# Storing a 16 KB result in two halves of 64 partitions, from SyncE and from ScalarE, in place of one store from SyncE

## The chip, the cores and the metric

One core of a Trainium2 chip. The metric is the device time of one execution in microseconds; a time quoted for a kernel is the median of several executions. Each experiment ran beside executions of the kernel before on the same chip. "Tail" means throughout: the time from the end of VectorE's last instruction to the end of the span, read from the trace of one profiled execution. It is the only stretch that the change touches, and in a trace it can be read to a few hundredths of a microsecond, while the whole time scatters by some tenths. The other terms: an "issue" is the time in which an engine's sequencer works on its store instruction. Beside the 128 rows of the store the trace has 16 closing writes of 4 bytes, and 16 "arrivals" are counted at the semaphore; with the last one the store has landed, and the time from the last row to it is called the confirmation.

## The reference

```python
batch, dim_i, dim_j, dim_k = 32, 256, 256, 128
x, y: (batch, 256) f32;  weight: (dim_k, dim_i, dim_j) f32      # 33.5 MB of weight
return np.einsum('bi,bj,kij->bk', x, y, weight)                 # (32, 128) f32: 16 KB
```

## The kernel before

The weight streams in through GpSimd's DMA queue and is cast to bf16 on the way; TensorE multiplies it with a block form of `x`, VectorE multiplies with `y` and sums. The result collects in `acc`: 128 partitions (a batch row and one of four groups of k on each), 32 numbers of 4 bytes on a partition. Partition p of `acc` is bytes 128p to 128p+127 of the result, so the store moves 128 rows of 128 bytes. The last unit's sum and the store:

```python
acc = sbuf("acc", [P, G], f32)                 # 128 x 32
# ... the last unit of weight rows:
done(v.tensor_tensor_reduce(
    out=prod[:, 0, :], in0=sums[:, 0, :], in1=y4, scale=1.0, scalar=0.0,
    op0=mult, op1=add, accum_out=acc[:, unit[0]:unit[0] + 1],
)._wait_ge(s_pe, n_pe))
# ...
out_v = out.rearrange("b (kk g) -> b kk g", kk=KK)
sp.dma_start(out=out_v, in_=acc)._wait_ge(s_dve, n_dve).then_inc(s_out, 16)
sp.sem_inc(s_fin, 1)
pool.wait_ge(s_fin, 1)
pool.dma_reset(range(nums[0], nums[-1] + 1))
pool.sem_clear(range(nums[0], nums[-1] + 1))
sp.wait_ge(s_out, 16)
sp.sem_clear(s_out)
```

SyncE waits for VectorE's last count, issues the store, tells GpSimd that it may clear the semaphores, then waits for the landing. ScalarE loads `x` and 1 MB of weight at the start, casts 2 MB, and has nothing to do after about 11 us.

Of the kernel before, what the change touches and what calls it, by code (L numbers as in the profile page):

```python
# [36 lines left out]
def kernel(  # L37
# [8 lines left out]
    P = 128  # L46
# [6 lines left out]
    B, I = x.shape  # L53
# [12 lines left out]
    def sbuf(name, shape, dtype):  # L66
        return nc.alloc_sbuf_tensor(name, shape, dtype).ap()

    def rows_of(groups):


        step = G // len(groups)
        assert all(g == groups[0] + n * step for n, g in enumerate(groups))
        v = weight.rearrange("(u s) (ip ic) j -> s ip u (ic j)", s=step, ic=IC)
        return v[groups[0]]

    def w_of(groups):
        at = [place_of[g] for g in groups]
        step = at[1] - at[0] if len(at) > 1 else 1
        assert all(a == at[0] + n * step for n, a in enumerate(at))  # L80
        return w_sb[:, at[0]:at[-1] + 1:step, :]
# [14 lines left out]
    acc = sbuf("acc", [P, G], f32)  # L96
# [6 lines left out]
        for s, (groups, lo, hi) in zip(s_w, LOADS) for g in groups for ic in range(lo, hi)  # L103
# [7 lines left out]
    s_dve = nc.alloc_semaphore("dve")  # L111
    s_fin = nc.alloc_semaphore("fin")
    s_out = nc.alloc_semaphore("out")
# [7 lines left out]
            out=w_of(groups)[:, :, lo * J:hi * J],  # L121
            in_=rows_of(groups)[:, :, lo * J:hi * J],
# [9 lines left out]
    for n, (g, queue) in enumerate(zip(FIRST, (nc.sync, nc.scalar))):  # L132
        hw.append(
            queue.dma_start(
                out=w_f[:, n:n + 1, :], in_=rows_of((g,)),
# [13 lines left out]
    for blk in blocks:  # L149
# [15 lines left out]
    pool, act, v, pe, sp = nc.gpsimd, nc.scalar, nc.vector, nc.tensor, nc.sync  # L165
# [4 lines left out]
        out=ident, in_=ident, compare_op=mybir.AluOpType.not_equal, fill=1.0,  # L170
# [13 lines left out]
    n_dve = 0  # L184

    def done(ins):
# [6 lines left out]
        out=x_rep,  # L193
        in_=x_sb.rearrange("b (ip ic) -> b ic ip", ic=IC).unsqueeze(3)
        .to_broadcast([B, IC, IP, KK]),
    )._wait_ge(s_x, 16))
    for q in range(Q):
        c = v.transpose(  # L198
            out=xt[q * 32:(q + 1) * 32, :, :],
            in_=x_rep[:, :, q * IP // Q:(q + 1) * IP // Q, :],  # L200
# [5 lines left out]
        out=mask, in_=ident.rearrange("p (ip kk) -> p kk ip", kk=KK), axis=AX, op=add,  # L206
    )._wait_ge(s_pool, 2))

    for kk in range(KK):
        c = v.tensor_scalar(  # L210
            out=xblk[:, :, :, kk], in0=xt, scalar1=mask[:, kk:kk + 1],
# [8 lines left out]
        out=yt, in_=y_sb.rearrange("b (jb j) -> b jb j", j=32),  # L220
    )._wait_ge(s_y, 16))
    t = done(v.tensor_copy(  # L222
        out=y_rep, in_=yt.unsqueeze(3).to_broadcast([B, J // 32, B, KK]),
    )._wait_ge(s_dve, t))
    BQ = B // Q
    for q in range(Q):
        c = v.transpose(  # L227
            out=y4[q * 32:(q + 1) * 32, :].rearrange("p (jb j) -> p jb j", j=32),
            in_=y_rep[:, :, q * BQ:(q + 1) * BQ, :],
# [22 lines left out]
    for u, unit in enumerate(UNITS):  # L252
# [40 lines left out]
        if n_g > 1:  # L293
            t = done(v.tensor_tensor(  # L294
                out=prod, in0=sums, in1=y4.unsqueeze(1).to_broadcast([P, n_g, J]), op=mult,
# [3 lines left out]
                out=acc[:, unit[0]:unit[-1] + 1:unit[1] - unit[0]], in_=prod, axis=AX, op=add,  # L299
            )._wait_ge(s_dve, t))  # L300
        else:
            done(v.tensor_tensor_reduce(  # L302
                out=prod[:, 0, :], in0=sums[:, 0, :], in1=y4, scale=1.0, scalar=0.0,
# [4 lines left out]


    out_v = out.rearrange("b (kk g) -> b kk g", kk=KK)  # L310
    sp.dma_start(out=out_v, in_=acc)._wait_ge(s_dve, n_dve).then_inc(s_out, 16)
    sp.sem_inc(s_fin, 1)
    pool.wait_ge(s_fin, 1)
    pool.dma_reset(range(nums[0], nums[-1] + 1))
    pool.sem_clear(range(nums[0], nums[-1] + 1))
    sp.wait_ge(s_out, 16)
    sp.sem_clear(s_out)


# [28 lines left out]
```

## Time and profile before

| | before |
|---|---|
| time, first three runs | 84.69, 84.77, 85.2 us; median 84.77 |
| span of the profiled run | 83.37 us |
| VectorE's last instruction ends | 81.87 us |
| tail | 1.50 us |
| from issue of the store to its landing | 1.4 us |

The first 81.9 us are set by the weight stream and what hangs on its last pieces; the tail is the store. The lines that show this are in the prediction below.

### The profile page before, as it was taken

To read this page: it belongs to the slowest core of one execution; us is meant where nothing else is said; L and a number is where in the kernel's file an instruction comes from. 1 tells how busy PE (TensorE), PEld (TensorE's weight loads), DVE (VectorE), ACT (ScalarE), POOL (GpSimd) and SP (SyncE) were. 2 spreads that over 40 slices of the span, in tenths; PEclk is the share of its full clock that TensorE was granted. 3 is DMA by queue.
4 is the path that set the end of the run, shared out by engine and by line. 5 is a ranking of instruction groups with operands and counts; after the bars stand their busy time and mean duration, and the time that the engine had idled before them with its cause. 6 is when DMAs were issued, how large, how long until landed. Compare 5 with 4: busy or idle time off the path is not lost.

```text
span 83.4 us, 257 instructions
## 1 busy us (share of the span) xinstructions
PE 32.5 (39%) x136; PEld 4.3 (5%) x43; DVE 25.2 (30%) x28; ACT 5.2 (6%) x5; POOL 8.8 (11%) x18
## 2 busy tenths in 40 slices
PE   0000000000000000000099999996029999884780
PEld 0000000000000000000000000000000110112330
DVE  0009450000292000000000000003999800999932
ACT  0019930000000000000000000000000000000000
POOL 5999600000000000000000000000000000000000
PEclk9999999999999999999999999999995799999998
DMA  4999999999999999999999999999999999999980
GB/s 122 393 370 293 214 214 212 216 218 212 218 218 216 212 216 216 212 218 214 212 214 218 210 220 214 214 214 216 212 214 218 212 214 216 212 216 214 197 118 8
DMA packets 4912, 17.91 MB, mean 215 GB/s; under 512 B 384, under 2 KB 800, under 8 KB 4656
## 3 DMA queue, kind: packets, MB, share of 16 engines
q0 software_dynamic: 4432, 15.76, 94.4%
q1 hardware_dynamic: 288, 1.07, 3.5%
q10 hardware_dynamic: 192, 1.08, 3.3%
HBM read 33.62 MB, written 0.02 MB: 403 GB/s over the span
## 4 chain that ended last, share of the span: by engine, by line
DMA 46%; PE 39%; DVE 6%; POOL 3%; another core or an unknown queue 3%; issue 2%; POOLq 0%
DMA w_sb<-in_weight_dram 46%; PE ps L237 39%; DVE tmp L294 5%; POOL w_sb L120 2%; POOL y_sb L127 1%; DVE tmp L302 1%; POOL const-float32-0.0 L332 0%; POOLq L332 0%; POOL const-uint8-127 L332 0%; POOL const-float32-1.0 L332 0%; DVE acc L302 0%
## 5 line engine op out<-in xcount | busy, mean ns | idle before, releaser
L237 PE MATMUL ps<-w_sb,xblk 128*128 128x512 bf16 (+1 forms) x136 | 32.5, 396 | 48.9 <-DMA w_sb<-in_weight_dram 44.2
L294 DVE TENSOR_TENSOR tmp<-ps,y 128x4096 f32<-128x4096 f32 (+3 forms) x4 | 8.6, 2156 | 36.7 <-PE ps L237 36.6
L298 DVE TENSOR_REDUCE acc<-tmp 128x16 f32<-128x4096 f32 (+3 forms) x4 | 8.6, 2154 | 0.1
L237 PEld LDWEIGHTS ps<-w_sb,xblk 128*128 128x128 bf16 x43 | 4.3, 101 | 76.9 <-DMA w_sb<-in_weight_dram 42.7
L120 POOL DMA_DIRECT2D w_sb<-in_weight_dram x11 | 7.6, 707 | 0.6 <-issue 0.6
L178 ACT CAST w_sb<-w_f 128x1024 bf16<-128x1024 f32 x4 | 3.9, 1040 | 0.0
L219 DVE STREAM_TRANSPOSE yt<-y_sb 32x256 f32<-32x256 f32 x1 | 0.4, 433 | 10.9 <-DMA y_sb<-in_y_dram 10.9
L192 DVE COPY x_rep<-x_sb 32x1024 f32<-32x1024 f32 x1 | 0.8, 790 | 6.1 <-PEq L332 6.1
L227 DVE STREAM_TRANSPOSE y<-y_rep 32x256 f32<-32x256 f32 x4 | 1.7, 435 | 0.1
L198 DVE STREAM_TRANSPOSE xt<-x_rep 32x256 f32<-32x256 f32 x4 | 1.7, 435 | 0.1
L178 ACT ACT_TABLE_LOAD x1 | 1.3, 1283 | 6.0 <-PEq L332 6.0
L210 DVE TENSOR_SCALAR xblk<-xt,mask 128x256 bf16<-128x256 f32 x4 | 1.4, 499 | 0.0
L302 DVE CUSTOM_DVE_ANT_0 tmp<-ps,y 128x256 f32<-128x256 f32 x2 | 0.8, 424 | 1.6 <-PE ps L237 1.6
L222 DVE COPY y_rep<-yt 32x1024 f32<-32x1024 f32 x1 | 0.7, 682 | 0.0
L205 DVE TENSOR_REDUCE mask<-ident 128x4 f32<-128x128 f32 x1 | 0.4, 382 | 1.0 <-POOL ident L169 1.0
L127 POOL DMA_DIRECT2D y_sb<-in_y_dram x1 | 0.5, 534 | 0.0
L168 POOL MEMSET ident<- 128x128 f32 x1 | 0.3, 302 | 0.0
L169 POOL TENSOR_SCALAR_AFFINE_SELECT ident<-ident 128x128 f32<-128x128 f32 x1 | 0.3, 287 | 0.1
L302 DVE DVE_READ_ACCUMULATOR2_ANT acc<- 128x1 f32 x2 | 0.2, 84 | 0.0
L332 POOL MEMSET const-float32-0.0<- 128x1 f32 x1 | 0.1, 98 | 0.2 <-issue 0.2
L332 POOL MEMSET const-bfloat16-1.0<- 128x1 bf16 x1 | 0.1, 101 | 0.0
L332 POOL MEMSET const-uint8-127<- 128x1 uint8 x1 | 0.1, 101 | 0.0
(1 smaller groups left out, 0.1 us busy)
## 6 DMA issues: line engine op xcount, KB each, us to landing
w_sb<-in_weight_dram POOLq DMA_DIRECT2D x2, 4096.0 KB, 48.0
w_sb<-in_weight_dram POOLq DMA_DIRECT2D x2, 2048.0 KB, 43.3
w_sb<-in_weight_dram POOLq DMA_DIRECT2D x2, 1024.0 KB, 40.9
w_f<-in_weight_dram SPq DMA_DIRECT2D x1, 1024.0 KB, 4.9
w_f<-in_weight_dram ACTq DMA_DIRECT2D x1, 1024.0 KB, 8.3
w_sb<-in_weight_dram POOLq DMA_DIRECT2D x1, 512.0 KB, 72.1
w_sb<-in_weight_dram POOLq DMA_DIRECT2D x1, 256.0 KB, 72.7
w_sb<-in_weight_dram POOLq DMA_DIRECT2D x1, 128.0 KB, 72.9
```

The source lines that it names most:

```text
L120: nc.gpsimd.dma_start(out=w_of(groups)[:, :, lo * J:hi * J], in_=rows_of(groups)[:, :, lo * J:hi * J],).then_inc(s, 16).ins
L127: sw.insert(2, nc.gpsimd.dma_start(out=y_sb, in_=y).then_inc(s_y, 16).ins)
L178: c = act.copy(out=w_sb[:, place_of[g], lo:hi], in_=w_f[:, n, lo:hi])
L192: t = done(v.tensor_copy(out=x_rep, in_=x_sb.rearrange("b (ip ic) -> b ic ip", ic=IC).unsqueeze(3) .to_broadcast([B, IC, IP, KK]),)._wait_ ...
L198: c = v.transpose(out=xt[q * 32:(q + 1) * 32, :, :], in_=x_rep[:, :, q * IP // Q:(q + 1) * IP // Q, :],)
L210: c = v.tensor_scalar(out=xblk[:, :, :, kk], in0=xt, scalar1=mask[:, kk:kk + 1], scalar2=None, op0=mult,)
L222: t = done(v.tensor_copy(out=y_rep, in_=yt.unsqueeze(3).to_broadcast([B, J // 32, B, KK]),)._wait_ge(s_dve, t))
L227: c = v.transpose(out=y4[q * 32:(q + 1) * 32, :].rearrange("p (jb j) -> p jb j", j=32), in_=y_rep[:, :, q * BQ:(q + 1) * BQ, :],)
L237: return pe.add_instruction(mybir.InstMatmult(name=nc.get_next_instruction_name(), engine=mybir.EngineType.PE, ins=[pe.lower_ap(rhs), pe.l ...
L294: t = done(v.tensor_tensor(out=prod, in0=sums, in1=y4.unsqueeze(1).to_broadcast([P, n_g, J]), op=mult,)._wait_ge(s_pe, n_pe))
L298: done(v.tensor_reduce(out=acc[:, unit[0]:unit[-1] + 1:unit[1] - unit[0]], in_=prod, axis=AX, op=add,)._wait_ge(s_dve, t))
L302: done(v.tensor_tensor_reduce(out=prod[:, 0, :], in0=sums[:, 0, :], in1=y4, scale=1.0, scalar=0.0, op0=mult, op1=add, accum_out=acc[:, uni ...
```

## The change

The intent: two engines issue half a store each at the same moment, so that each half is ready sooner.

```diff
-    sp.dma_start(out=out_v, in_=acc)._wait_ge(s_dve, n_dve).then_inc(s_out, 16)
+    act.dma_start(out=out_v[B // 2:], in_=acc[P // 2:, :])._wait_ge(s_dve, n_dve).then_inc(s_out, 16)
+    act.sem_inc(s_fin, 1)
+    sp.dma_start(out=out_v[:B // 2], in_=acc[:P // 2, :])._wait_ge(s_dve, n_dve).then_inc(s_out, 16)
     sp.sem_inc(s_fin, 1)
-    pool.wait_ge(s_fin, 1)
+    pool.wait_ge(s_fin, 2)
     ...
-    sp.wait_ge(s_out, 16)
+    sp.wait_ge(s_out, 32)
```

## The prediction

> **What bounds the kernel now.** The question put to each view was: how much of the time lies behind the last addition, because only that stretch can change. I read first the page's header and slices, then the chain of waits, then the timeline of the last microseconds, then the waits of SyncE, and last the engine table cut into short windows. First the page.
>
> ```profile
> span 83.4 us, 257 instructions
> PE   0000000000000000000099999996029999884780
> DMA  4999999999999999999999999999999999999980
> GB/s 122 393 370 293 214 214 212 216 218 212 218 218 216 212 216 216 212 218 214 212 214 218 210 220 214 214 214 216 212 214 218 212 214 216 212 216 214 197 118 8
> ```
>
> Look at the DMA row: from the second slice to the 38th the DMA engines are at 90% or more, at some 215 GB/s, and TensorE starts only in the second half. The weight stream sets the pace; each slice is 2.1 us, so the stream's end falls near 81 us. The last slice, with DMA 0 and 8 GB/s, is where the result leaves. The chain of waits shows what stands between the stream and that slice:
>
> ```profile
> 3.18 38.65 DMA w_sb<-in_weight_dram
> 41.87 15.66 PE ps L237 x64
> ...
> 81.12 0.30 PE ps L237
> 81.42 0.02 issue
> 81.44 0.42 DVE tmp L302
> 81.86 0.01 DVE acc L302
> ```
>
> The reader should see that the chain ends at 81.87 us, on VectorE, while the span is 83.4 us (83.37 in the trace). The remaining 1.5 us belong to the store, which the chain does not list because a store is no counted work. The changed lines act on these 1.5 us, 1.8% of the 84.77 us. The timeline and SyncE's own waits fill them:
>
> ```profile
> 81.79 0.08 DVE L302 DVE_READ_ACCUMULATOR2_ANT acc<- 128x1 f32 x1
> 81.90 0.35 SPq L311 DMA_DIRECT2D out_dram<-acc  x1
> SPq L317 <- DMA out_dram<-acc: 1.0, 1, 1.0
> out_dram<-acc SPq DMA_DIRECT2D x1, 16.0 KB, 1.4
> ```
>
> SyncE issues for 0.35 us, then waits 1.0 us for the landing; from issue to landing it is 1.4 us for 16 KB. Cutting that stretch into windows shows when bytes move (columns: window, length, busy times, then granted clock, DMA share, GB/s):
>
> ```profile
> 81.90:82.25 0.35, 0.00 (x0) 0.00 (x0) 0.00 (x0) 0.00 (x0) 0.00 (x0) 1.00 0.00 0
> 82.25:82.72 0.47, 0.00 (x0) 0.00 (x0) 0.00 (x0) 0.00 (x0) 0.00 (x0) 1.00 0.00 0
> 82.72:82.98 0.26, 0.00 (x0) 0.00 (x0) 0.00 (x0) 0.00 (x0) 0.00 (x0) 0.71 0.42 63
> 82.98:83.33 0.35, 0.00 (x0) 0.00 (x0) 0.00 (x0) 0.00 (x0) 0.00 (x0) 0.50 0.00 0
> ```
>
> So: 0.02 us from VectorE's end to the issue, 0.35 us issue, 0.47 us with no byte moving, 0.26 us in which all 128 rows of 128 bytes go, 0.35 us from the last row to the semaphore, 0.04 us until SyncE has cleared it. Sum 1.49 us. Bytes move in only 0.26 of it, and even there the 16 engines are busy 0.42 of the time, 0.11 us each (8 rows of 13 ns in the trace's packet records). Behind the span comes a fixed remainder: the profiled run took 84.67 us for 83.37 us of span, 1.30 us.
>
> **What the Trainium skill says.** Four places bear on it.
> "DMA: Bandwidth & Descriptors", section "Rules for kernel authors", has this very change: two transfers to disjoint partition halves, "Don't bother — they serialize", because both halves spread over all 16 DMA engines. Its section "Issuing engines are not separate DMA queues" allows one saving: issuing from several engines "will only save the time on the sequencer it takes to initiate the DMA". Section "Anatomy of one DMA" puts nearly all of a transfer's fixed cost (about 2 us there, for transfers issued by GpSimd) into waiting for the write to be confirmed, not into moving bytes. The trace agrees in kind: 16 KB take 1.4 us, of which 0.26 move data; but the confirmation, 0.35 us, is the smaller part here, and issue plus the silent gap, 0.82 us, the larger.
> "Perfetto Trace Analysis", section "Per-instruction lifecycle", says that the block which writes the descriptors is shared by the two issuing sequencers and locked for one DMA at a time, and that this lock wait lies inside the reported issue window. Whether two issues lengthen each other here is the open question. At the start of this trace SyncE issues from 0.00 for 0.63 us and ScalarE from 0.12 for 0.42 us; they overlap, and ScalarE ends first. So a long strict exclusion is not what is seen, but 0.42 us for only 32 rows, against 0.35 us for the lone store's 128, would fit some mutual hindrance (or the cold start of both).
>
> **The change part by part.**
> Removed: nothing but the size of SyncE's store, 128 rows to 64. Its issue could get shorter if the 0.35 us grew with rows. The trace speaks against much of that: 32 rows took 0.42 us, 128 rows 0.35, 0.56 and 0.63 us. No order by rows is in these four. I put the saving at 0 to 0.05 us.
> Added: one issue on ScalarE of 64 rows. ScalarE's last counted instruction (a cast) ends at about 11.2 us, so its store instruction stands waiting for VectorE's last count for 70 us, as SyncE's does, and both should be released together at about 81.90 us. It lies beside SyncE's issue, so its cost on the path is 0 unless they hinder each other.
> The silent gap, 0.47 us: paid by both stores at once; no saving, it is latency.
> The data: each engine still gets 8 rows, now 4 from each queue, plus 2 closing semaphore writes in place of 1 (9 ns each in the packet records). 0.26 us stays 0.26, perhaps 0.27 us. At the kernel's start, ScalarE's 1 MB transfer sent its first packet at 4.19 us, just as SyncE's 1 MB was sending its last (4.22 us): two queues ran one after the other, not side by side. For 4 rows an engine that makes no sum smaller.
> The confirmation, 0.35 us: the wait is now for the later of two transfers, so the larger of two such latencies counts. Of one transfer's sixteen arrivals the trace has the first at 83.15 and the last at 83.33 us; a maximum over 32 instead of 16 lands a few hundredths later: plus 0 to 0.05 us.
> Moved: GpSimd now clears semaphores after both issues. In the trace it does so from 82.33 to 82.59 us, with SyncE busy waiting until 83.33; it has 0.7 us to spare, so a slightly later start costs nothing.
> Untouched: all up to 81.87 us, and the 1.30 us behind the span.
> Sum: 0 to -0.05 (issue), 0 (gap), +0.01 (data), 0 to +0.05 (confirmation): about 0.00 us if the two issues run freely side by side.[...]
>
> **The rivals.**
> First: the two issues truly overlap and both issue and gap are shorter for 64 rows. For it: a half has half the descriptors to write, and part of the 0.82 us before the first byte may be that writing. Against it: the issue lengths show no such order. If issue and gap both shrank by a quarter it would be -0.2 us, 84.57 us. I give this, or part of it, 20%.
> Second: the lock makes the later store wait for the earlier one. Then the second issue ends up to one issue later: at worst +0.35 us, 85.12 us, and more likely a part of it, +0.1 to +0.2 us. For it: the skill's shared block, and the 0.42 us for 32 rows. Against it: the overlap at the start. I give 35% to some visible hindrance.
> Third: nothing to see, the change drowns in the scatter between runs (84.69 to 85.2 us, 0.5 us among three runs of one kernel): 45%.
> A fourth, that GpSimd's clearing becomes the end, would need its start delayed by more than its 0.7 us of slack; under 3%.
> What none of these can do is reach 2%, 1.70 us: the whole stretch that is touched is 1.49 us, so even a store costing nothing would not do it, and a doubled store (two in strict sequence, issue to landing 1.4 us twice) would be +1.4 us, still within.
>
> **Range and chances.** Weighted: 0.20 × -0.15 + 0.35 × +0.17 + 0.45 × 0 = +0.03, plus the few hundredths for the later of two landings: +0.05 us, so 84.82 us. The mechanism alone spans about -0.2 to +0.35 us; run scatter of the weight stream's end adds some 0.2 us either way, and a median of few runs keeps part of that. I take 84.50 to 85.20 us for 8 in 10. Faster by over 2% (under 83.07 us): 1%. Slower by over 2% (over 86.47 us): 1%, for a different state of the chip rather than for the change. Within 2%: 98%.
>
> **What would show each step right or wrong.** The page should list two issues with 8 KB each, one of SPq and one of ACTq, starting within 0.05 us of each other at about 0.02 us after VectorE's end. Packets should rise by exactly 16, from 4912 to 4928: the rows are the same 128, and one more set of closing writes is added (queue q1 down by 64 to 224, q10 up by 80 to 272). If both issues last about 0.35 us, hindrance is refuted; if one lasts 0.5 us or more, or starts its bytes only when the other's are done with a gap, the second rival is shown. The data phase should stay within 0.23 to 0.35 us at GB/s like before's 63. SyncE's wait for the landing should be 0.9 to 1.2 us. The tail from VectorE's end to the span's end should be 1.4 to 1.8 us, against 1.49. What would make the prediction wrong: a chain up to VectorE's end that differs by more than 0.3 us from 81.87 (then the stream moved, which the change does not explain), a silent gap that grows well over 0.47 us when two queues start at once, or an issue on ScalarE late by more than 0.2 us because its sequencer is slower to wake after 70 us.

## The result, and the profile after

The changed kernel took 85.39 us (median of 6 runs, 85.29 to 85.49), the kernel before 84.80 us (6 runs, 84.69 to 85.2). The ratio is 1.0062, with a 95% interval from 1.0039 to 1.0084: slower by about 0.5 us, small but clear. All six runs were fast, that is, none was over 1.5% above the fastest.

The timeline's last lines and SyncE's wait, after:

```profile
81.96 0.08 DVE L302 DVE_READ_ACCUMULATOR2_ANT acc<- 128x1 f32 x1
82.07 0.52 SPq L313 DMA_DIRECT2D out_dram<-acc  x1
82.07 0.55 ACTq L311 DMA_DIRECT2D out_dram<-acc  x1
SPq L319 <- DMA out_dram<-acc: 1.4, 1, 1.4
out_dram<-acc SPq DMA_DIRECT2D x1, 8.0 KB, 1.7
out_dram<-acc ACTq DMA_DIRECT2D x1, 8.0 KB, 2.0
```

Both engines start together, 0.03 us after VectorE's end, as they should. But each issue now takes 0.52 or 0.55 us where the whole store's took 0.35, and half the bytes take 1.7 and 2.0 us to land where the whole took 1.4. The windows of the tail (columns as in the prediction):

```profile
82.07:82.62 0.55, 0.00 (x0) 0.00 (x0) 0.00 (x0) 0.00 (x0) 0.00 (x0) 1.00 0.00 0
82.62:83.24 0.62, 0.00 (x0) 0.00 (x0) 0.00 (x0) 0.00 (x0) 0.00 (x0) 1.00 0.00 0
83.24:83.45 0.21, 0.00 (x0) 0.00 (x0) 0.00 (x0) 0.00 (x0) 0.00 (x0) 1.00 0.27 39
83.45:83.51 0.06, 0.00 (x0) 0.00 (x0) 0.00 (x0) 0.00 (x0) 0.00 (x0) 1.00 0.00 0
83.51:83.72 0.21, 0.00 (x0) 0.00 (x0) 0.00 (x0) 0.00 (x0) 0.00 (x0) 1.00 0.28 39
83.72:84.06 0.34, 0.00 (x0) 0.00 (x0) 0.00 (x0) 0.00 (x0) 0.00 (x0) 1.00 0.00 0
```

Rows move twice, in two bursts with a pause of 0.06 us between them. By the packet records the first burst is SyncE's and the second ScalarE's. Counted from VectorE's end:

| | before | after | difference |
|---|---|---|---|
| first row leaves | 0.871 us | 1.203 us | +0.332 |
| first row to end of the last closing write | 0.234 us | 0.477 us | +0.243 |
| last closing write to last arrival at the semaphore | 0.349 us | 0.336 us | -0.013 |
| last arrival to end of span | 0.042 us | 0.046 us | +0.004 |
| tail | 1.496 us | 2.062 us | +0.566 |

The 0.566 us are the whole of the ratio (0.62% of 84.8 us is 0.53 us). VectorE's end also lies 0.17 us later in this trace (82.04 against 81.87), but so does the landing of the last weights (81.24 against 81.07); over the fifteen profiled runs that add nothing to the weight stream VectorE's end falls between 81.74 and 82.22 us, so that is scatter of the stream. GpSimd's clearing ends 0.92 us after VectorE's end, over a microsecond before the span's end.

From here on "last row" includes its closing write, which ends 5 to 6 ns after the rows.

Three questions follow. Why is the first row later? Why do two halves not move side by side? And is either a matter of two engines at all?

### The profile page after: what moved, and what is told of

Read it like the earlier page. It is cut to its first block, busy times and chain, and to the rows that moved or that the text cites. A ratio compares the mean times of both kernels' runs of the same rounds, so it can differ in the third digit from the quotient of the medians.

```text
span 84.1 us, 259 instructions
## 1 busy us (share of the span) xinstructions
PE 33.4 (40%) x136; PEld 4.3 (5%) x43; DVE 25.0 (30%) x28; ACT 5.3 (6%) x5; POOL 8.8 (10%) x18
## 2 busy tenths in 40 slices
DMA packets 4928, 17.91 MB, mean 213 GB/s; under 512 B 400, under 2 KB 816, under 8 KB 4672
## 4 chain that ended last, share of the span: by engine, by line
DMA 46%; PE 40%; DVE 6%; POOL 3%; another core or an unknown queue 2%; issue 1%; POOLq 0%
DMA w_sb<-in_weight_dram 46%; PE ps L237 40%; DVE tmp L294 5%; POOL w_sb L120 2%; POOL y_sb L127 1%; DVE tmp L302 1%; POOL const-float32-0.0 L334 0%; POOLq L334 0%; POOL const-uint8-127 L334 0%; POOL const-float32-1.0 L334 0%; DVE acc L302 0%
## 5 line engine op out<-in xcount | busy, mean ns | idle before, releaser
L237 PE MATMUL ps<-w_sb,xblk 128*128 128x512 bf16 (+1 forms) x136 | 33.4, 405 | 48.2 <-DMA w_sb<-in_weight_dram 43.5
```

Source lines behind the costliest of these rows:

```text
L237: return pe.add_instruction(mybir.InstMatmult(name=nc.get_next_instruction_name(), engine=mybir.EngineType.PE, ins=[pe.lower_ap(rhs), pe.l ...
```

## The experiments

Fifteen kernels ran, on four chips. Those marked "alone" store only a part and give a wrong result. Nine of the fifteen were run once, for their trace; only the lengths within their tails are used, not their times. The diffs below are cut to the lines that matter: lines that they replace, and waits that only count along, are partly left out.

### First round: is it the two engines, ScalarE, the second transfer, or the half?

Theory A, the leading one, was the second rival of the prediction: two issues at the same moment hinder each other. Theory B: ScalarE's store is slow in itself, or the 64-row form is. Theory C: any second transfer costs this much.

**e1_both_sync**: both halves by SyncE.

```diff
-    sp.dma_start(out=out_v, in_=acc)._wait_ge(s_dve, n_dve).then_inc(s_out, 16)
+    sp.dma_start(out=out_v[:B // 2], in_=acc[:P // 2, :])._wait_ge(s_dve, n_dve).then_inc(s_out, 16)
+    sp.dma_start(out=out_v[B // 2:], in_=acc[P // 2:, :]).then_inc(s_out, 16)
     ...
-    sp.wait_ge(s_out, 16)
+    sp.wait_ge(s_out, 32)
```

> Both 64-row halves issued by SyncE, one after the other. Theory A (two issues at the same moment hinder each other): without a second engine each issue is back at 0.35 us, the second starts 0.35 to 0.40 us after the first, its rows follow the first half's rows directly, and the tail from VectorE's end to the span's end is 1.49 + 0.39 - 0.03 = 1.85 us, so about 85.15 us, less than the 85.39 us of the two-engine store. Theory C (any second transfer costs half a microsecond, whoever issues it): tail 2.06 us, about 85.4 us. Theory B (ScalarE's queue is slow): tail near 1.85 us too, so A and B are told apart by the other runs.

Measured: correct, 85.74 us against 84.82, ratio 1.0114 (1.0086 to 1.0143); tail 2.40 us. None of the theories had this. The issues, from the timeline:

```profile
82.14 0.50 SPq L311 DMA_DIRECT2D out_dram<-acc  x1
82.68 0.59 SPq L312 DMA_DIRECT2D out_dram<-acc  x1
```

No second engine is near, and yet the first issue takes 0.50 us and the second 0.59. Theory A fails its first test here.

**e2_scalar_whole**: the whole store by ScalarE.

```diff
-    sp.dma_start(out=out_v, in_=acc)._wait_ge(s_dve, n_dve).then_inc(s_out, 16)
-    sp.sem_inc(s_fin, 1)
+    act.dma_start(out=out_v, in_=acc)._wait_ge(s_dve, n_dve).then_inc(s_out, 16)
+    act.sem_inc(s_fin, 1)
```

> The whole 128-row store issued by ScalarE alone, as SyncE did before. Theory A: as before, issue 0.35 us, first row 0.84 us after the start of the issue, tail 1.5 us, 84.8 us. Theory B (a store on ScalarE is slow in itself, after 70 us of idleness): issue 0.55 us, first row 1.2 us after the start of the issue or later, tail 1.8 us or more, 85.1 us or more.

Measured: correct, 84.95 us against 84.82, ratio 1.0008 (0.9989 to 1.0026); issue 0.38 us, first row at 0.92 us, tail 1.55 us. ScalarE is 0.05 us slower than SyncE from end to end, no more. Waking after 70 idle microseconds costs nothing that shows.

**e3_half_alone**: SyncE's 64 rows alone.

```diff
-    sp.dma_start(out=out_v, in_=acc)._wait_ge(s_dve, n_dve).then_inc(s_out, 16)
+    sp.dma_start(out=out_v[:B // 2], in_=acc[:P // 2, :])._wait_ge(s_dve, n_dve).then_inc(s_out, 16)
```

> SyncE stores its 64 rows, nobody stores the other 64 (a wrong result on purpose). Theory A: issue 0.35 us, first row at 0.84 us, rows all out within 0.2 us, tail 1.46 us, 84.75 us: the half itself costs what the whole costs. If the 64-row form itself is what takes 0.52 us to issue (theory B for the form), the issue stays at 0.52 us and the tail at 1.8 us, 85.1 us.

Measured: wrong; 85.15 us against 84.82, ratio 1.0034 (1.0018 to 1.0050); tail 1.80 us. Storing half of the result alone is slower than storing all of it. The issue from the timeline, then the windows of the gap and of the rows:

```profile
82.00 0.53 SPq L311 DMA_DIRECT2D out_dram<-acc  x1
```

```profile
82.52:83.17 0.65, 0.00 (x0) 0.00 (x0) 0.00 (x0) 0.00 (x0) 0.00 (x0) 1.00 0.00 0
83.17:83.38 0.21, 0.00 (x0) 0.00 (x0) 0.00 (x0) 0.00 (x0) 0.00 (x0) 1.00 0.27 39
```

Issue 0.53 us, first row at 1.205 us after VectorE's end: just the numbers of the changed kernel's first burst (0.52 and 1.203), with nobody beside it. So the +0.33 us before the first row come from the 64-row transfer, not from two engines meeting. Theory A is dead for that part. The rest of the change, 2.06 - 1.80 = 0.26 us, is the second burst.

**e4_staggered**: ScalarE starts when SyncE has issued.

```diff
+    sp.dma_start(out=out_v[:B // 2], in_=acc[:P // 2, :])._wait_ge(s_dve, n_dve).then_inc(s_out, 16)
     sp.sem_inc(s_fin, 1)
+    act.dma_start(out=out_v[B // 2:], in_=acc[P // 2:, :])._wait_ge(s_fin, 1).then_inc(s_out, 16)
+    act.sem_inc(s_fin, 1)
```

> As the changed kernel, but ScalarE waits until SyncE has finished its issue. Theory A: both issues are back at 0.35 us, ScalarE's starts about 0.43 us after SyncE's, tail 1.46 + 0.43 = 1.9 us, 85.2 us: starting later ends no later or even sooner than the 2.06 us and 85.39 us of the simultaneous issue. Theory B: SyncE's issue stays 0.52 us and ScalarE's starts after it, tail 2.4 us or more, 85.7 us.

Measured: correct, 85.70 us against 84.82, ratio 1.0099 (1.0082 to 1.0116); tail 2.39 us. This is what theory B said. The issues, and the window of ScalarE's rows:

```profile
82.03 0.52 SPq L311 DMA_DIRECT2D out_dram<-acc  x1
82.62 0.52 ACTq L313 DMA_DIRECT2D out_dram<-acc  x1
83.80:84.01 0.21, 0.00 (x0) 0.00 (x0) 0.00 (x0) 0.00 (x0) 0.00 (x0) 0.50 0.28 39
```

Apart in time or together, a 64-row issue takes 0.52 to 0.55 us, and together is better than apart. But the two do hinder each other after the issue. Here ScalarE's first row leaves 1.18 us after the start of its issue (83.80 - 82.62), just as SyncE's does (1.17 us here, 1.18 in the changed kernel and in e3_half_alone). In the changed kernel, where both issue at once, ScalarE's first row leaves 1.44 us after the start of its issue (83.51 - 82.07): 0.26 us later. So theory A, dead for the first burst, holds for the start of the second. What holds the rows back there, no run shows. (ScalarE's half with no other store at all was not run.)

### Second round: what about 64 rows is slow?

Theory D: only the full 128 partitions are quick. Theory F: small transfers are slow. Theory G: the issue grows as rows become fewer.

**e5_columns_two**: both engines at once, split by columns.

```diff
+    act.dma_start(out=out_v[:, :, G // 2:], in_=acc[:, G // 2:])._wait_ge(s_dve, n_dve).then_inc(s_out, 16)
+    act.sem_inc(s_fin, 1)
+    sp.dma_start(out=out_v[:, :, :G // 2], in_=acc[:, :G // 2])._wait_ge(s_dve, n_dve).then_inc(s_out, 16)
```

> The result split between SyncE and ScalarE by columns instead of by partitions: each stores 128 rows of 64 bytes, the same 8 KB each as in the changed kernel. Theory D (a store over all 128 partitions has a quicker issue than one over 64, whatever its bytes): both issues 0.35 to 0.38 us, first row 0.87 us after VectorE's end, the second engine's rows follow the first's, tail 1.50 + 0.26 = 1.76 us, about 85.1 us. Theory F (small transfers of 8 KB are slow to issue): both issues 0.52 us, first row at 1.2 us, tail 2.06 us, 85.4 us. Theory A in what is left of it (two engines hinder each other): issues well over 0.38 us although the rows are 128.

Measured: correct, 85.06 us against 84.86, ratio 1.0029 (1.0005 to 1.0053); tail 1.67 us. The issues, and then the windows of rows and of the confirmation:

```profile
82.10 0.35 SPq L313 DMA_DIRECT2D out_dram<-acc  x1
82.10 0.38 ACTq L311 DMA_DIRECT2D out_dram<-acc  x1
```

```profile
82.94:83.22 0.28, 0.00 (x0) 0.00 (x0) 0.00 (x0) 0.00 (x0) 0.00 (x0) 1.00 0.64 59
83.22:83.70 0.48, 0.00 (x0) 0.00 (x0) 0.00 (x0) 0.00 (x0) 0.00 (x0) 0.66 0.00 0
```

The same two engines, the same 8 KB each, the same moment: and the issues take 0.35 and 0.38 us, what each engine took alone (0.35 before, 0.38 in e2_scalar_whole). So at these counts two issues do not hinder each other visibly, and bytes are not what makes an issue slow (theory F falls). The rows of the two queues leave side by side here (0.88 to 1.10 us and 0.93 to 1.15 us after VectorE's end), in 0.28 us together, where theory D had expected them one after the other and a tail of 1.76 us. What a second store still costs is 0.18 us: the last row 0.05 us later, and 0.13 us more until the last arrival (0.48 us instead of 0.35).

**e6_rows_96** and **e7_rows_32**: 96 and 32 rows alone.

```diff
-    sp.dma_start(out=out_v, in_=acc)._wait_ge(s_dve, n_dve).then_inc(s_out, 16)
+    sp.dma_start(out=out_v[:96 // KK], in_=acc[:96, :])._wait_ge(s_dve, n_dve).then_inc(s_out, 16)
```

(and the same with 32 in place of 96)

> SyncE stores 96 of the 128 partitions, nothing else is stored (a wrong result on purpose). Theory D (only the full 128 is quick): issue 0.52 us and first row at 1.2 us after VectorE's end, as with 64. Theory G (the issue grows steadily as rows become fewer): issue half way, 0.43 us, first row at 1.04 us.

> SyncE stores 32 of the 128 partitions, nothing else (wrong on purpose). Theory D: issue 0.52 us and first row at 1.2 us, as with 64. Theory G: issue 0.6 us, first row at 1.37 us. If fewer rows in the slow form do save work, issue under 0.5 us.

Measured: issue 0.354 and 0.352 us, first row at 0.876 and 0.873 us, tail 1.48 and 1.44 us. Both as quick as 128. Theories D and G are both refuted: the kernel with 32 rows and that with 64 differ in a single number, and the smaller and the larger counts are quick while the one between is slow.

**e8_64_by_2**: 64 partitions, two pieces of 60 bytes from each.

```diff
+    sp.dma_start(
+        out=out_v[:B // 2].rearrange('b kk (h g) -> (b kk) h g', h=2)[:, :, :15],
+        in_=acc[:P // 2, :].rearrange('p (h g) -> p h g', h=2)[:, :, :15],
+    )._wait_ge(s_dve, n_dve).then_inc(s_out, 16)
```

> SyncE stores 64 partitions, each in two pieces of 60 bytes, so 128 pieces in all from half the partitions (wrong on purpose). Theory D with partitions as what counts: issue 0.52 us or more, first row at 1.2 us. If it is the number of pieces, or the count on the side of the memory, that makes the quick form: issue 0.35 us, first row at 0.87 us.

Measured: issue 0.57 us, first row at 1.25 us, tail 1.87 us. 128 pieces from 64 partitions are slow too; on the memory's side this transfer counts 128 rows, so it is the 64 on the partitions' side that goes with the slowness. (One run; pieces of 60 bytes from another number of partitions were not tried.)

### Third round: is it exactly 64, and does moving the border help?

Theory H: 64 is a bad count among good ones.

**e9_96_and_32**: the change with its border at partition 96.

```diff
+    act.dma_start(out=out_v[24:], in_=acc[96:, :])._wait_ge(s_dve, n_dve).then_inc(s_out, 16)
+    act.sem_inc(s_fin, 1)
+    sp.dma_start(out=out_v[:24], in_=acc[:96, :])._wait_ge(s_dve, n_dve).then_inc(s_out, 16)
```

> The change with another border: SyncE stores partitions 0 to 95, ScalarE 96 to 127, at the same moment. Theory H (64 rows are a bad count, 32 and 96 are good ones): issues 0.35 and 0.38 us, first rows at 0.87 and 0.93 us after VectorE's end, tail 1.55 to 1.67 us, 84.95 to 85.05 us, so two thirds of the loss gone with the border alone. If the loss came from two engines storing different partitions at once: issues over 0.5 us, tail 2.0 us, 85.4 us.

Measured: correct, 85.06 us against 84.78, ratio 1.0037 (1.0016 to 1.0058); tail 1.67 us. The issues:

```profile
82.06 0.35 SPq L313 DMA_DIRECT2D out_dram<-acc  x1
82.06 0.38 ACTq L311 DMA_DIRECT2D out_dram<-acc  x1
```

This is the changed kernel with nothing different but where the cut lies, and its tail is 0.39 us shorter (1.67 against 2.06). It equals the split by columns, and it is still 0.17 us longer than the single store.

**e10_64_from_32**, **e11_rows_60**, **e12_rows_48**, all alone:

```diff
+    sp.dma_start(out=out_v[32 // KK:96 // KK], in_=acc[32:96, :])...      # e10
+    sp.dma_start(out=out_v[0 // KK:60 // KK], in_=acc[0:60, :])...        # e11
+    sp.dma_start(out=out_v[0 // KK:48 // KK], in_=acc[0:48, :])...        # e12
```

> SyncE stores partitions 32 to 95 alone (wrong on purpose): 64 rows that neither start nor end at the middle. Theory H (the count): issue 0.52 us, first row at 1.2 us, tail 1.8 us. If what counts is that the slow stores lay within one half of the partitions: issue 0.35 us, first row at 0.87 us, tail 1.46 us.

> SyncE stores 60 of the 128 partitions alone (wrong on purpose). If the slow form belongs to four rows for each DMA engine, as 64 rows on 16 engines and 60 rows on 15 engines have: issue 0.52 us, first row at 1.2 us, and 15 closing writes instead of 16. If it belongs to 64 exactly: issue 0.35 us or a little more, first row at 0.87 to 0.95 us.

> SyncE stores 48 of the 128 partitions alone (wrong on purpose), three rows for each engine. Theory H (64 is singular): issue 0.35 us, first row at 0.87 us, tail 1.45 us. If a whole range between 32 and 96 is slow: issue 0.45 us or more, first row at 1.0 us or later.

Measured: partitions 32 to 95, issue 0.57 us, first row at 1.26 us, tail 1.84 us. 60 rows, issue 0.41 us, first row at 0.87 us, tail 1.42 us. 48 rows, issue 0.35 us, first row at 0.88 us, tail 1.44 us. So 64 rows are slow in all three places tried, 48 and 60 are not. The 60 rows have 15 closing writes (75 packets in all), so they went over 15 DMA engines, four rows for each as with 64 rows and 16 closing writes: four rows for an engine is not the reason either. Their issue is 0.06 us longer than 0.35, without the first row being later, and one of the sixteen arrivals at the semaphore comes at 0.56 us, 0.12 us after the end of the issue and 0.3 us before any row. This agrees with the Trainium skill, "DMA: Bandwidth & Descriptors", section "Why a DMA increments its semaphore by 16 and not by 1": the issuing sequencer writes itself the counts of the engines that take no part.

### Last round: other counts, loads, and the confirmation of two stores

**e13_store_counts** and **e14_load_counts**: eleven small transfers in SyncE's idle time, each waited for before the next.

```diff
+    sp.wait_ge(s_f[0], 16)                                      # e13 only: w_f has landed
+    for n_probe, n in enumerate((128, 64, 32, 64, 96, 80, 112, 48, 16, 64, 128)):
+        sp.dma_start(out=out_v[:n // KK], in_=w_f[:n, 0, :G]).then_inc(s_probe, 16)         # e13
+        sp.dma_start(out=scratch[:n, :], in_=x.rearrange('b (c e) -> (b c) e', e=32)[:n]).then_inc(s_probe, 16)   # e14
+        sp.wait_ge(s_probe, 16 * (n_probe + 1))
     sp.dma_start(out=out_v, in_=acc)._wait_ge(s_dve, n_dve).then_inc(s_out, 16)
```

> The kernel before with eleven small stores added on SyncE in the long stretch where it is idle, of 128, 64, 32, 64, 96, 80, 112, 48, 16, 64 and 128 rows of 128 bytes, each waited for before the next; the real store overwrites what they wrote. Theory H (64 is singular): the issues of 64 rows take 0.5 to 0.6 us all three times, all others about 0.35 us. If 64 is one of several bad counts, 16, 80 or 112 are over 0.45 us too. If the slow issue has to do with the end of the kernel or the result's tile, 64 is like the others here.

> The same eleven counts as loads of rows of 128 bytes into an unused tile. If the slow issue belongs to the count of 64 in any direction: 0.5 to 0.6 us for 64 rows, about 0.35 us for the others. If it belongs to stores: 64 rows take about 0.35 us as the others.

Both correct. The stores, in the order of the list above (start and length of each issue, from the timeline):

```profile
6.04 0.35 SPq L314 DMA_DIRECT2D out_dram<-w_f  x1
12.91 0.51 SPq L314 DMA_DIRECT2D out_dram<-w_f  x1
19.17 0.35 SPq L314 DMA_DIRECT2D out_dram<-w_f  x1
24.53 0.47 SPq L314 DMA_DIRECT2D out_dram<-w_f  x1
30.63 0.32 SPq L314 DMA_DIRECT2D out_dram<-w_f  x1
37.33 0.32 SPq L314 DMA_DIRECT2D out_dram<-w_f  x1
43.54 0.32 SPq L314 DMA_DIRECT2D out_dram<-w_f  x1
49.98 0.32 SPq L314 DMA_DIRECT2D out_dram<-w_f  x1
55.17 0.31 SPq L314 DMA_DIRECT2D out_dram<-w_f  x1
59.60 0.47 SPq L314 DMA_DIRECT2D out_dram<-w_f  x1
65.29 0.35 SPq L314 DMA_DIRECT2D out_dram<-w_f  x1
```

The second, fourth and tenth are the 64-row ones: 0.51, 0.47 and 0.47 us. All others, 16, 32, 48, 80, 96, 112 and 128 rows, take 0.31 to 0.35 us. The loads give the same picture: 0.50, 0.47 and 0.47 us for 64 rows, 0.31 to 0.36 us for the rest. Among the multiples of 16 up to 128, 64 alone is slow, in both directions, for another source tile and long before the kernel's end. Theory H stands in every test, though 0.47 us is a little under the 0.5 to 0.6 us expected, and counts beside 64 were tried no nearer than 60 and 80. Why it is 64, no run shows. (Their landings and their times are not to be compared: they run inside the weight stream, and VectorE ends later, near 82.5 us.)

**e15_two_counts**: the split by columns, each store with its own semaphore.

```diff
-    act.dma_start(... in_=acc[:, G // 2:])._wait_ge(s_dve, n_dve).then_inc(s_out, 16)
+    act.dma_start(... in_=acc[:, G // 2:])._wait_ge(s_dve, n_dve).then_inc(s_out2, 16)
     ...
+    sp.wait_ge(s_out2, 16)
```

> The split by columns again, each store with its own completion semaphore. If the shared semaphore stretches the confirmation: the last arrival comes 0.35 us after the last row, not 0.48. If the confirmation of two stores in flight is longer whatever counts it: again 0.45 to 0.5 us.

Measured: correct; the last row ends at 1.154 us after VectorE's end and the last arrival is at 1.670 us, 0.52 us later, a little more than the 0.45 to 0.5 us expected. The shared semaphore is not the reason. (The tail is 1.84 us, longer than with one semaphore because SyncE now waits and clears twice after the last arrival.) The trace now tells the two stores apart: SyncE's arrivals fall between 1.29 and 1.51 us, ScalarE's between 1.46 and 1.67 us, 13 to 20 ns apart, although ScalarE's rows were only 0.05 us behind. So the confirmation of the second store runs largely behind that of the first. What makes them queue stays open.

## Why the prediction was wrong, by its own steps

**The bound, and the reach of the change: right.** All that changed lies in the tail, and the effect stayed within 2%. The forecast of 4928 packets, of 224 and 272 on the two queues, of two 8 KB issues starting within 0.05 us of each other: as seen. Of its signs, SyncE's wait for the landing (0.9 to 1.2 us, seen 1.4), the data phase (0.23 to 0.35 us, seen 0.48) and the tail (1.4 to 1.8 us, seen 2.06) failed.

**The step that failed: "Removed: ... I put the saving at 0 to 0.05 us".** It took the issue of 64 rows for at most as long as that of 128, since the four lengths that the trace offered showed no order by rows. They showed none, but they held no transfer of 64 rows, and they gave no leave to interpolate. The first rival, issue and gap both shorter for 64 rows, had the sign reversed. The issue of 64 rows is 0.17 us longer (0.52 for 0.35), and with it the next term went wrong: "The silent gap, 0.47 us: ... no saving, it is latency". It is not a constant; the gap grew by another 0.16 us, from 0.49 to 0.66 us by the packet records (the prediction's windows put the first row 0.02 us early). Together +0.33 us before the first row, and e3_half_alone shows the half alone doing this, with a tail 0.30 us longer.

**The data: "0.26 us stays 0.26, perhaps 0.27": it grew by 0.24 us, from 0.23 to 0.48.** The reasoning, that each DMA engine still has 8 rows, holds only if the second queue's rows are ready when the first's are done. Two 64-row transfers issued together put their first rows 0.27 us apart; two quick ones 0.05 to 0.06 us apart (e5_columns_two, e9_96_and_32). The test apart in time (e4_staggered) shows that 0.26 us of the delay of ScalarE's rows come from the two issues meeting; the quick counts show that meeting does no such harm there. So it takes both: 64 rows, and two issues at once.

**The confirmation, "plus 0 to 0.05 us": right for the change** (-0.01 us), because the two halves' rows come one after the other and the first is confirmed meanwhile (sixteen arrivals by 1.76 us, sixteen more from 1.85 us on). It is 0.13 us wrong where the rows do come side by side.

**The second rival, hindrance between two issues: right in part, and not where the prediction looked first.** The prediction said that an issue of 0.5 us or more would show it. It does not: a length can be long for another reason, and here it was. With quick counts two simultaneous issues take 0.352 and 0.377 us, and 0.350 and 0.380 alone. The test that could decide was the half alone, which a profile of the changed kernel can't give. The prediction's other sign, bytes that start only when the other's are done, with a gap, was seen (0.06 us), and there the rival holds: 0.26 us of ScalarE's wait for its first row. Whether a lock causes it is not shown, and the forecast "+0.1 to +0.2 us" was meant for a longer issue.

**What carried no weight: ScalarE waking late** (it started 0.005 us after SyncE), GpSimd's clearing, and the stretch behind the span, 1.30 us before and 1.34 us after.

In numbers, the 0.57 us are: 0.17 us for a second store at all (the tail of e9_96_and_32, 1.67, less 1.50) and 0.39 us for both stores having 64 rows (2.06 less 1.67). Of the 0.39, 0.30 us are the late first store (e3_half_alone, 1.80 less 1.50). An estimate from these differences leaves 0.09 us for the two 64-row stores meeting: ScalarE's rows are held back by 0.26 us, but a second store confirmed after the first costs less than two confirmed together (0.34 against 0.48 us). No split that was tried beats the single store, and there is little to win: even 32 rows alone leave a tail of 1.44 us, 0.06 us under that of all 128. No correct kernel here is faster than the kernel before; the whole store from ScalarE cannot be told from it.

## What to carry to other kernels

This 16 KB store at the end of a kernel is nearly all latency (rows move in 0.23 of its 1.50 us): cutting it into pieces saved nothing, and the second piece has its own cost, here 0.17 us. When a small transfer behaves oddly, run the part alone and vary its count by one step each way before blaming the engines that share the work: here 48, 60, 80 and 96 rows were quick, and the natural half, 64, was not. A length read in one profile shows that something takes long; only a run that leaves out the suspected partner, or moves it away in time, shows who is to blame. And look past the issue: the two engines' issues were hardly longer together, yet ScalarE's rows came 0.26 us later.

## What the Trainium skill lacked or had wrong

- "DMA: Bandwidth & Descriptors" has nothing on an issue's time by its number of rows. Here, on SyncE, 64 rows of 128 bytes took 0.47 to 0.53 us to issue for a store (0.57 us for partitions 32 to 95, 0.59 us for the second of two in a row), 0.47 to 0.50 us for a load; 16, 32, 48, 80, 96, 112 and 128 rows took 0.31 to 0.36 us. In the tail the first row then left at 1.2 us instead of 0.87 us.
- The same page, section "Rules for kernel authors", is right that two stores to disjoint halves are not worth it. Its reason, that they serialize, holds here only for 64 rows (two bursts, 0.06 us apart). With 96 and 32 rows, or 128 and 128, the rows of both queues left side by side, within 0.26 to 0.28 us, and the loss of 0.17 to 0.18 us was mostly in the confirmation: 0.48 to 0.49 us from the last row to the last arrival, against 0.35 us for one store.
- The same page, section "Anatomy of one DMA", divides the fixed cost for transfers issued by GpSimd alone, with most of it in the confirmation of the write. For this store, issued by SyncE, the division is another: issue and the silence before the first row were 0.84 us, the confirmation 0.35 us.
- "Perfetto Trace Analysis", section "Per-instruction lifecycle", describes a lock wait between the two issuing engines inside the issue window. With quick counts none was visible: 0.352 and 0.377 us together, 0.350 and 0.380 us alone. With 64 rows on both engines the delay lay after the issue: issues of 0.52 and 0.55 us, but ScalarE's first row 1.44 us after the start of its issue, against 1.18 us when it issued apart.
